# A hybrid decoder layer on one core: one group's block sums formed in device memory

## The chip, the cores and the metric

One core of a Trainium2 chip runs the whole layer as one program. The metric is the device time of one execution in microseconds. TensorE (PE) does the matrix products, VectorE (DVE) and ScalarE (ACT) the elementwise work, GpSimd (POOL) a few tiny operations and the accumulating transfers, SyncE (SP) issues plain transfers. The 16 DMA engines are shared by all queues. A transfer issued from POOL can add to its destination (`accum_op=ALU.add`); here these are called accumulates.

## The reference, cut to what matters

A decoder layer on 256 tokens of width 1024, all in fp32: a projection, block-sparse attention beside retention, an output projection, cross attention into 256 memory rows, and a gated FFN of inner width 2816, each with norms:

```python
h = rms_norm(x, g_pre_ffn[l])
gu = h @ w_gate_up[l]
f = (jax.nn.silu(gu[..., :D_FF]) * gu[..., D_FF:]) @ w_down[l]
x = x + rms_norm(f, g_post_ffn[l])
```

The change concerns the product with `w_gate_up`.

## The kernel before, in words

All weights lie in one array `weights` of blocks of 128 x 1024 fp32 (512 KB). Each block is used as two parts, high and low: ACT writes the high part (a copy to the rounded format, line 195), DVE the rest (line 196, a subtraction); this is a *split*, made by `split_weight`. PE then makes three products for each pair of operands (high x high, high x low, low x high). The blocks have numbers q in the order in which they are split (the table `SPLIT` sets it for the FFN); PE uses them in the order of `USE`. Split blocks lie in a ring of nine buffers, `hl`.

A block comes to its split in one of two ways. A *plain* one (kind `"w"`) is loaded by SP into a ring of six buffers, `raw`; `load_weight` issues the load for a later block when a split has freed a buffer. The others are *home* blocks, which stay in one of three tiles, `kT`, `qv` and `ret`, in SBUF.

Home blocks exist because of the *seven-product groups* 1 to 4. Each group covers 512 columns of the gate and of the up half for both tiles of 128 tokens. In place of eight products of quarter size, seven are made, from sums and differences of the quarters. With the quarters 11, 12, 21, 22, the weight operands are: product 1: 11; 2: 21; 3: 22; 5: 11+12; 7: 22+12 (with the signs taken in by the token operands); 6: 11+12+22; 4: 11+12+22+21. Each operand has two blocks (parts). Products of a group have the PE line 1167, with the accumulators x, y and z.

In a group the homes are loaded with three quarters and then changed in place: after its split a home block gets another quarter added, either by DVE (line 202, where the other quarter lies in a home) or by an accumulate that POOL issues (line 204). `load_home` (line 145) makes the first loads; group 1's are issued by SP, those of the later groups by POOL once the group before has read the home for the last time.

Side work (norms, softmax, the kernel's tails of a product) is written as generators that `run_side` resumes at numbered steps of PE's program; `late` starts some at a fixed step, and `WAIT` holds the delays in steps. A split is put off by a step in which side work was resumed, unless it is due. So a new generator can also move splits. All engines run their own instructions in order, and SP and POOL stop at a transfer that has to wait.

Of the kernel before, what the change touches and what calls it, by code (L numbers as in the profile page):

```python
# [7 lines left out]
F32 = mybir.dt.float32  # L8
F32R = mybir.dt.float32r
BF16 = mybir.dt.bfloat16  # L10
AF = mybir.ActivationFunctionType
ALU = mybir.AluOpType
AX = mybir.AxisListType

P = 128
D = 1024
# [6 lines left out]
FFN_Q = 64  # L23
HOMES = {1: ('kT', 'qv', 'ret', '21'), 2: ('qv', 'kT', 'ret', '21'), 3: ('qv', 'kT', 'ret', '21'), 4: ('qv', 'kT', 'ret', '12')}
SEVEN = tuple(HOMES)
# [2 lines left out]
USE = 'r20 r21 d0 d1 1:1 d2 1:2 1:5 1:6 1:3 d3 1:7 d20 1:4 2:1 d21 2:2 d4 2:5 2:6 2:3 2:7 d5 2:4 3:1 3:2 d6 d7 d9 d8 3:5 3:6 3:3 3:7 d10 3:4 d11 d12 d13 4:1 d14 4:2 4:5 4:6 4:3 4:7 d15 4:4'.split()  # L28
SPLIT = 'r20 r21 d0 1:1 d1 1:2 d2 1:5 1:3 1:6 d3 1:7 1:4 d20 2:1 2:2 d21 d4 2:5 2:3 2:6 2:4 2:7 d5 3:2 3:1 d6 d9 d7 d8 3:5 3:3 3:6 3:4 3:7 d10 d12 d11 d13 d14 4:1 4:5 4:2 4:6 4:3 d15 4:7 4:4'.split()
DOWN_END = (16, 17, 18, 19)  # L30
FIRST_OUT = (0, 512, 768, 1024)
ROW_TILES = tuple(int(what[1:]) for what in USE if what[0] == "r")
ROWS_AT = FFN_Q + 8
SEVEN_AT = ROWS_AT + 2 * len(ROW_TILES)
DOWN_AT = SEVEN_AT + 8 * len(SEVEN)

WAIT = {
    "cpb0": 2, "cpb1": 1, "cpv0": 7, "cpv1": 1, "cu0": 3, "cu1": 4, "ex_c0": 2, "ex_c1": 1, "ex_m00": 0,
    "ex_m10": 0, "ex_m11": 4, "f0_0": 8, "f0_1": 7, "g_add": 0, "g_silu": 5, "gate0": 3, "gate1": 6,
    "gp1": 5, "gp2": 0, "k_add": 0, "k_hl": 3, "lag": 2, "ret": 12, "low": 6, "mq": 0, "mrow": 3, "ms": 21, "mst": 5,  # L40
# [14 lines left out]
def tile_hybrid_layer(  # L55
# [14 lines left out]
    nc = tc.nc  # L70
# [3 lines left out]
    hlp = ctx.enter_context(tc.tile_pool(name="hlp", bufs=RING))  # L74
    rawp = ctx.enter_context(tc.tile_pool(name="rawp", bufs=RAW))
    stp = ctx.enter_context(tc.tile_pool(name="stp", bufs=1))
    t2k = ctx.enter_context(tc.tile_pool(name="t2k", bufs=7))
    p4 = ctx.enter_context(tc.tile_pool(name="p4", bufs=2))
    pt4 = ctx.enter_context(tc.tile_pool(name="pt4", bufs=3))
# [42 lines left out]
    emitted = set()  # L122

    def need(*keys):

        missing = [k for k in keys if k not in emitted]
        assert not missing, missing
# [7 lines left out]
    raws, hls = {}, {}  # L135

    items = [("w", q) for q in range(FFN_Q)]
    queue = []
    sums = {}

    def load_home(engine, g, home, part, w):

# [4 lines left out]
    def load_weight():  # L147

        if not queue:
            return  # L150
        q = queue.pop(0)
        kind, w = items[q][:2]
        if kind == "w":
            raws[q] = rawp.tile([P, D], F32, tag="raw", name=f"raw{q}")
            nc.sync.dma_start(raws[q], weights[w])
        else:
            for key in firsts[q]:
                if key[:2] not in follows:
                    load_home(nc.sync, *key)
            load_weight()  # L160

    homes = {}
    ringed = []
    split_at = {}
    ret_kept = [1000, 1000]
    beside = {}
    firsts, follows, released = {}, {}, {}

    def free_home(q, i):

        if len(ringed) < RING or last_use[ringed[-RING]] + WAIT["lag"] <= i:
            return "hl"
        if q >= FFN_Q and ("oT", 7, 1) in emitted:
            for tag in ("qv", "kT", "ret") if q < FFN_Q + 8 else ("ret",) if not ret_kept[0] - WAIT["ret"] < q <= ret_kept[1] else ():
                if tag not in homes or last_use[homes[tag]] + WAIT["lag"] <= i:
                    return tag
        return None

    def split_weight(q, parts=1, home="hl"):
        kind = items[q][0]  # L180
        if kind == "w":
            raw = raws.pop(q)
        else:
            g, tag, part = items[q][2:5]
            raw = sums[(g, tag)][:, part, :]
        if home == "hl":
            ringed.append(q)
            h = hlp.tile([P, 2, D], F32R, tag="hl", name=f"hl{q}")
        else:
            homes[home] = q  # L190
            h = actp.tile([P, 2, D], F32R, tag=home, name=f"hl{q}")
        w = D // parts
        for i in range(parts):
            n = slice(i * w, (i + 1) * w)
            nc.scalar.activation(h[:, 0, n], raw[:, n], AF.Copy)  # L195
            nc.vector.tensor_tensor(out=h[:, 1, n], in0=raw[:, n], in1=h[:, 0, n].bitcast(F32), op=ALU.subtract)  # L196
        hls[q] = h
        split_at[q] = step_no[0]
        if kind != "w":
            plus, more = items[q][5:7]  # L200
            if plus is not None:
                nc.vector.tensor_tensor(out=raw, in0=raw, in1=sums[(g, plus)][:, part, :], op=ALU.add)  # L202
            if more is not None:
                nc.gpsimd.dma_start(raw, weights[more], accum_op=ALU.add)
            for key in released.get(q, ()):
                load_home(nc.gpsimd if HOME_LOADS == "late-pool" else nc.sync, *key)
        if kind == "w":
            load_weight()
# [456 lines left out]
    parts = {}  # L665
# [154 lines left out]
    both = [(0, 1)]  # L820
# [45 lines left out]
    def seven_items(g, w0):  # L866

        b = {"11": w0, "12": w0 + 2, "21": w0 + 4, "22": w0 + 6}
        one, two, three = HOMES[g][:3]
        held = HOMES[g][3] if three else None  # L870
        here = g in ON_CHIP
        plus = {1: three if held == "12" else None, 5: two if here else None, 6: three if held == "21" else None,
                3: three if held == "12" else None}
        more = {1: "12", 5: "22", 6: "21", 3: "12"}
        chain = {m: (kind, w, home, plus.get(m), None if plus.get(m) else more.get(m))
                 for m, kind, w, home in ((1, "first", "11", one), (3, "first", "22", two), (5, "sum", None, one),
                                          (6, "sum", None, one), (7, "sum", None, two), (4, "sum", None, one))}
        if held == "21":
            chain[2] = ("first", "21", three, None, None)
        if held == "12":  # L880
            for part in range(2):
                beside[(g, one, part)] = (three, b["12"] + part)
        made = {(2, part): ("w", b["21"] + part) for part in range(2)}
        for m, (kind, source, home, plus, more) in chain.items():
            for part in range(2):
                made[(m, part)] = (kind, b[source] + part if source else None, g, home, part, plus,
                                   None if more is None else b[more] + part, m)
        return made
# [6 lines left out]
    place = {}  # L895
    made = {g: seven_items(g, SEVEN_AT + 8 * n) for n, g in enumerate(SEVEN)}
    for what in SPLIT + [f"d{k}" for k in DOWN_END]:
        if what[0] == "r":
            w = ROWS_AT + 2 * ROW_TILES.index(int(what[1:]))
# [5 lines left out]
    for what in USE:  # L905
# [4 lines left out]
        elif what[0] == "d":  # L910
            k = int(what[1:])
# [8 lines left out]
    for half in range(2):  # L920
        for q, k in blocks:
            steps.append(("down", q, 1, k // 4, k % 4, (half,)))
    NQ = len(items)
    kept = [q for q, item in enumerate(items) if item[0] != "w" and "ret" in (item[3], item[5])]
    if kept:
        ret_kept[:] = kept[0], kept[-1]

    loads, last_read = {}, {}
    for q, item in enumerate(items):
        if item[0] == "w":  # L930
            continue
        kind, w, g, home, part, plus = item[:6]
# [41 lines left out]
    qv = actp.tile([P, 2048], F32, tag="qv", name="qv")  # L974
# [72 lines left out]
    raw = raws.pop(0)  # L1047
# [12 lines left out]
    split_weight(1, 2)  # L1060
    x_split(2, 3)
    opening = {4: lambda: x_split(4, 5), 7: lambda: x_split(6, 7)}
    late = {WAIT["xd"]: x_load, WAIT["xs"]: x_stats, WAIT["ms"]: mem_stats}
    pending_split = list(range(2, NQ))

    accs, downs = {}, {}
    for i, s in enumerate(steps):
# [14 lines left out]
        if i == starts["ffn"]:  # L1082
            f = stp.tile([P, 2, 2, 4, 256], F32R, tag="stB", name="fT")
            T["fT"] = f
        if s[0] == "first":

            _, q, c = s
            need(("xT", q, 0))
            h = hls[q][:, :, c * 512:(c + 1) * 512]
# [211 lines left out]
```

## Time and profile before

| | |
|---|---|
| median of 3 timed runs | 400.16 us (399.66 to 400.49) |
| profiled execution | 398.5 us, of which the span is 396.7 us |
| PE busy | 389.1 us of the span |
| DVE busy | 320.5 us |
| ACT busy | 257.6 us |
| TensorE clock granted | 0.999 |
| SP queue (q1) | 62.97 MB, 45.1% of the DMA engines' span |
| POOL queue (q0) | 16.78 MB, 17.1% |

Stages, by the profile: input projection with attention and retention to about 111 us, keys and queries of the cross attention to 156 us, its values and output to about 215 us, FFN from there. A row of instructions has the line, engine, operation, output and inputs by the program's names, the form, the count, and the busy time or start; a share of DMA is the mean over the 16 engines.

### The profile page before, as it was taken

How to read it: one execution, taken by the hardware profiler on the slowest of the kernel's cores; microseconds unless marked ns; L12 is line 12 of the kernel's file. 1: busy time of each engine (PE TensorE's matmuls, PEld its weight loads, DVE VectorE, ACT ScalarE, POOL GpSimd, SP SyncE). 2: the span in 40 equal slices, each digit the busy share in tenths (PEclk: the TensorE clock that was granted, in tenths of full speed). 3: DMA queues.
4: the chain of work that ended last, by engine and by line, in shares of the span. 5: the costliest groups of instructions: out<-in, count | busy, mean ns of one | idle time of the engine just before them, and what ended most of it. 6: DMA issues, size and time to landing. Idle time of an engine off the chain costs nothing.

```text
span 396.7 us, 5465 instructions
## 1 busy us (share of the span) xinstructions
PE 389.1 (98%) x1969; PEld 323.8 (82%) x1969; DVE 320.5 (81%) x447; ACT 257.6 (65%) x431; POOL 33.4 (8%) x53
## 2 busy tenths in 40 slices
PE   8999999999999999999999999999999999999993
PEld 5888777888889888888988888888888888888882
DVE  4875976686869977677576699998999799999964
ACT  5786973964757865494547765757758685647641
POOL 0010010200011000000001001022113103101000
PEclk9999999999999999999999999999999999999999
DMA  8998746367546676607271459968949878935202
GB/s 280 415 401 274 253 159 212 106 207 275 168 152 240 184 218 204 213 6 240 74 265 55 159 191 359 299 104 315 241 120 274 245 241 178 366 146 121 40 0 106
DMA packets 23067, 80.36 MB, mean 203 GB/s; under 512 B 2560, under 2 KB 3072, under 8 KB 23040
## 3 DMA queue, kind: packets, MB, share of 16 engines
q1 hardware_dynamic: 18288, 62.97, 45.1%
q0 software_dynamic: 4608, 16.78, 17.1%
q8 instruction: 15, 0.25, 0.2%
q10 hardware_dynamic: 144, 0.26, 0.2%
q14 instruction: 12, 0.10, 0.1%
HBM read 78.95 MB, written 1.05 MB: 202 GB/s over the span
## 4 chain that ended last, share of the span: by engine, by line
PE 91%; DVE 3%; issue 2%; ACT 1%; DMA 1%; POOL 1%; DVEq 0%; POOLq 0%; ACTq 0%
PE x L1167 11%; PE acc L1107 11%; PE acc L1109 11%; PE acc L1108 11%; PE acc L1131 9%; PE y L1167 5%; PE acc L1134 5%; PE down L1152 5%; PE down L1154 5%; PE down L1153 5%; PE acc L1095 3%; PE z L1167 3%; DVE hl L196 1%; DMA raw<-in_weights_dram 1%; PE c_f L658 1%
## 5 line engine op out<-in xcount | busy, mean ns | idle before, releaser
L196 DVE TENSOR_TENSOR hl<-raw,hl 128x1024 fp32r<-128x1024 f32 (+1 forms) x102 | 119.3, 1189 | 16.9 <-ACT hl L195 16.8
L195 ACT ACTIVATE hl<-raw 128x1024 fp32r<-128x1024 f32 (+1 forms) x102 | 102.6, 1031 | 1.1 <-DMA raw<-in_weights_dram 1.0
L195 ACT ACTIVATE hl<-sum_qv 128x1024 fp32r<-128x1024 f32 x28 | 29.1, 1056 | 16.6 <-DVE sum_qv L202 12.1
L196 DVE TENSOR_TENSOR hl<-sum_qv,hl 128x1024 fp32r<-128x1024 f32 x28 | 34.0, 1220 | 1.4 <-ACT hl L195 1.3
L1107 PE MATMUL acc<-hl,xT 128*128 128x512 f32 x80 | 32.9, 411 | 0.0
L1109 PE MATMUL acc<-hl,xT 128*128 128x512 f32 x80 | 31.3, 392 | 0.0
L1152 PE MATMUL down<-hl,fT 128*128 128x512 f32 x80 | 31.3, 392 | 0.0
L1108 PE MATMUL acc<-hl,xT 128*128 128x512 f32 x80 | 31.2, 390 | 0.0
L1154 PE MATMUL down<-hl,fT 128*128 128x512 f32 x80 | 31.2, 390 | 0.0
L1153 PE MATMUL down<-hl,fT 128*128 128x512 f32 x80 | 31.2, 389 | 0.0
L196 DVE TENSOR_TENSOR hl<-sum_kT,hl 128x1024 fp32r<-128x1024 f32 x20 | 24.1, 1220 | 0.7 <-ACT hl L195 0.7
L1167 PE MATMUL x<-hl,x2T 128*128 128x512 f32 x96 | 23.2, 393 | 0.0
L1167 PE MATMUL x<-hl,comb 128*128 128x512 f32 x96 | 23.1, 390 | 0.0
L1167 PE MATMUL y<-hl,comb 128*128 128x512 f32 x96 | 23.1, 389 | 0.0
L1167 PEld LDWEIGHTS x<-hl,comb 128*128 128x128 f32 x96 | 17.9, 188 | 3.9 <-DVE hl L196 0.2
L1167 PEld LDWEIGHTS y<-hl,comb 128*128 128x128 f32 x96 | 18.0, 188 | 3.7
L195 ACT ACTIVATE hl<-sum_kT 128x1024 fp32r<-128x1024 f32 x20 | 20.5, 1051 | 0.5 <-DMA sum_kT<-in_weights_dram 0.5
L1167 PEld LDWEIGHTS x<-hl,x2T 128*128 128x128 f32 x96 | 17.7, 188 | 3.7 <-DVE s L685 0.2
L1154 PEld LDWEIGHTS down<-hl,fT 128*128 128x128 f32 x80 | 15.0, 188 | 3.3 <-DVE fT L661 0.2
L1109 PEld LDWEIGHTS acc<-hl,xT 128*128 128x128 f32 x80 | 15.0, 188 | 3.3
L1107 PEld LDWEIGHTS acc<-hl,xT 128*128 128x128 f32 x80 | 15.1, 189 | 3.1 <-issue 0.3
L1152 PEld LDWEIGHTS down<-hl,fT 128*128 128x128 f32 x80 | 15.0, 188 | 3.0
(258 smaller groups left out, 856.8 us busy)
## 6 DMA issues: line engine op xcount, KB each, us to landing
raw<-in_weights_dram SPq DMA_DIRECT2D x98, 512.0 KB, 4.9
sum_qv<-in_weights_dram POOLq DMA_DIRECT2D x14, 512.0 KB, 5.8
sum_kT<-in_weights_dram POOLq DMA_DIRECT2D x12, 512.0 KB, 6.8
sum_ret<-in_weights_dram POOLq DMA_DIRECT2D x6, 512.0 KB, 4.2
gpost<-in_gpost_dram SPq DMA_DIRECT2D x3, 512.0 KB, 4.9
x_sb<-in_x_dram SPq DMA_DIRECT2D x2, 512.0 KB, 8.2
memn<-in_mem_dram SPq DMA_DIRECT2D x2, 512.0 KB, 7.5
mr<-in_memT_dram SPq DMA_DIRECT2D x2, 512.0 KB, 7.4
```

The lines of the kernel that those rows point to most:

```text
L195: nc.scalar.activation(h[:, 0, n], raw[:, n], AF.Copy)
L196: nc.vector.tensor_tensor(out=h[:, 1, n], in0=raw[:, n], in1=h[:, 0, n].bitcast(F32), op=ALU.subtract)
L1095: nc.tensor.matmul(accs[(c, t)], T["xT"][:, hx, q, tok(t)], h[:, hw, :], start=begin, stop=False)
L1107: nc.tensor.matmul(acc, xh, h[:, 0, kk, :], start=(first and kk == 0), stop=False)
L1108: nc.tensor.matmul(acc, xh, h[:, 1, kk, :], start=False, stop=False)
L1109: nc.tensor.matmul(acc, xl, h[:, 0, kk, :], start=False, stop=(last and kk == 1))
L1131: nc.tensor.matmul(acc, hls[q][:, 0, k * P:(k + 1) * P], T[f"{st}_k"][:, k, :], start=begin, stop=end, skip_group_check=True)
L1134: nc.tensor.matmul(acc[:, 0:256], hls[q][:, 1, k * P:(k + 1) * P], T[st][:, 0, k, :], start=begin, stop=end, skip_group_check=True)
L1152: nc.tensor.matmul(acc, fh, wh, start=first, stop=False, skip_group_check=True)
L1153: nc.tensor.matmul(acc, fh, wl, start=False, stop=False, skip_group_check=True)
L1154: nc.tensor.matmul(acc, fl, wh, start=False, stop=last, skip_group_check=True)
L1167: nc.tensor.matmul(acc, a, h[:, w, kk, :], start=begin and kk == 0 and n == 0, stop=end and n == 2, skip_group_check=True)
```

## The change

Group 1 has no home blocks any more: all of its operands are plain blocks. Its sums are made ahead in device memory, in four scratch tensors of two blocks each. The new generator `make_sums` starts at step 70 (some 118 us in). For each sum it issues a copy of a quarter, or of an earlier sum, from device memory to device memory on SP, and later an accumulate of another quarter into the copy on POOL. The order is `PRE_ORDER`: copies for 5 and 7, accumulates for 5 and 7, copy of 5 to 6, accumulate of 22 into 6, copy of 6 to 4, accumulate of 21 into 4; two parts each, so eight copies and eight accumulates. A copy is followed by a delay of two steps, an accumulate by one of three. The blocks are then loaded through `raw` like weights (14 loads).

```diff
-FIRST_OUT = (0, 512, 768, 1024)
+PRE = (1,)
+PRE_ON = "sp"
+PRE_ORDER = "c5 c7 a5 a7 c6 a6 c4 a4".split()
+FIRST_OUT = (0, 256, 512, 640, 768, 1024)
...
 WAIT = {
+    "pre": 70, "pc": 2, "pa": 3,
...
+    dramp = ctx.enter_context(tc.tile_pool(name="dramp", bufs=1, space=bass.MemoryType.DRAM))
...
+    def make_sums():
+        for g in PRE:
+            at = SEVEN_AT + 8 * SEVEN.index(g)
+            w0 = {"11": at, "12": at + 2, "21": at + 4, "22": at + 6}
+            for what in PRE_ORDER:
+                m = int(what[1])
+                source, plus = {5: ("11", "12"), 7: ("22", "12"), 6: (5, "22"), 4: (6, "21")}[m]
+                for part in range(2):
+                    key = (g, m, part)
+                    if what[0] == "c":
+                        if part == 0:
+                            both = dramp.tile([P, 2, D], F32, tag=f"sum{g}{m}", name=f"sum{g}{m}")
+                        made_sums[key] = both[:, part, :]
+                        engine = nc.sync if PRE_ON == "sp" else nc.gpsimd
+                        engine.dma_start(made_sums[key], block((g, source, part) if isinstance(source, int) else w0[source] + part))
+                    else:
+                        nc.gpsimd.dma_start(made_sums[key], weights[w0[plus] + part], accum_op=ALU.add)
+                        emitted.add(("sum",) + key)
+                    yield WAIT["pc"] if what[0] == "c" else WAIT["pa"]
...
         if kind == "w":
+            if not isinstance(w, int):
+                need(("sum",) + w)
             raws[q] = rawp.tile([P, D], F32, tag="raw", name=f"raw{q}")
-            nc.sync.dma_start(raws[q], weights[w])
+            nc.sync.dma_start(raws[q], block(w))
...
     def seven_items(g, w0):
         b = {"11": w0, "12": w0 + 2, "21": w0 + 4, "22": w0 + 6}
+        if g in PRE:
+            plain = {1: "11", 2: "21", 3: "22"}
+            return {(m, part): ("w", b[plain[m]] + part if m in plain else (g, m, part)) for m in range(1, 8) for part in range(2)}
...
-    late = {WAIT["xd"]: x_load, WAIT["xs"]: x_stats, WAIT["ms"]: mem_stats}
+    late = {WAIT["pre"]: make_sums, WAIT["xd"]: x_load, WAIT["xs"]: x_stats, WAIT["ms"]: mem_stats}
```

`block(w)` gives `weights[w]` for a number and the scratch tensor for a key. `FIRST_OUT` cuts the output of the first token tile into pieces of columns. The rule by which a split may use a free home as a tenth buffer is also written for each home apart; the places in which it is used stay the same (three blocks of the first FFN products).

The order of PE's instructions does not change at all. Three places on the queues and on DVE do. SP, in the stage of the cross attention's queries and values, from before:

```order
L155 DMA raw_1532<-in_weights_dram 128x1024
L155 DMA raw_1555<-in_weights_dram 128x1024
L155 DMA raw_1586<-in_weights_dram 128x1024
L155 DMA raw_1609<-in_weights_dram 128x1024
L155 DMA raw_1640<-in_weights_dram 128x1024
```

and now (`sum_1262` holds operand 5, `sum_1579` operand 6, `sum_1714` operand 4):

```order
L188 DMA raw_1544<-in_weights_dram 128x1024
L188 DMA raw_1567<-in_weights_dram 128x1024
L166 DMA sum_1579<-sum_1262 128x1024
L188 DMA raw_1600<-in_weights_dram 128x1024
L166 DMA sum_1579<-sum_1262 128x1024
L188 DMA raw_1624<-in_weights_dram 128x1024
L188 DMA raw_1656<-in_weights_dram 128x1024
L188 DMA raw_1683<-in_weights_dram 128x1024
L188 DMA raw_1695<-in_weights_dram 128x1024
L188 DMA raw_1706<-in_weights_dram 128x1024
L166 DMA sum_1714<-sum_1579 128x1024 x2
L188 DMA raw_1824<-in_weights_dram 128x1024
```

Two copies for operand 6 (each waits for an accumulate into `sum_1262`) and two for operand 4 (each waits for one into `sum_1579`) now stand ahead of raw loads that only waited for a buffer. The load of before at the place of `raw_1600` was issued at 149.86 us, that at the place of `raw_1824` at 163.88 us.

POOL, from the first norm of the mixer to the cross attention's second norm, now (`sum_1323` holds operand 7):

```order
L258 TENSOR_TENSOR r_x_1279<-v_x_1277,mhalf 128x1
L168 DMA sum_1262<-in_weights_dram 128x1024 x2
L168 DMA sum_1323<-in_weights_dram 128x1024 x2
L168 DMA sum_1579<-in_weights_dram 128x1024 x2
L168 DMA sum_1714<-in_weights_dram 128x1024 x2
L258 TENSOR_TENSOR r_p_cross_2091<-v_p_cross_2089,mhalf 128x1
```

Before, `r_p_cross` followed `r_x` directly; now eight accumulates, which wait for SP's copies, stand between.

DVE in group 1, from the splits of operand 5 to those of operand 6, before:

```order
L196 TENSOR_TENSOR hl_2546<-sum_kT_2236,hl_2546 128x1024
L202 TENSOR_TENSOR sum_kT_2236<-sum_kT_2236,sum_qv_2317 128x1024
L196 TENSOR_TENSOR hl_2556<-sum_kT_2236,hl_2556 128x1024
L202 TENSOR_TENSOR sum_kT_2236<-sum_kT_2236,sum_qv_2317 128x1024
L196 TENSOR_TENSOR hl_2567<-sum_qv_2317,hl_2567 128x1024
L535 TENSOR_TENSOR f_2577<-sg_2429,f_2577 128x256
L614 TENSOR_TENSOR sg_2483<-sg_2483 128x256
L196 TENSOR_TENSOR hl_2589<-sum_qv_2317,hl_2589 128x1024
L196 TENSOR_TENSOR hl_2599<-sum_kT_2236,hl_2599 128x1024
L202 TENSOR_TENSOR sum_kT_2236<-sum_kT_2236,sum_ret_2282 128x1024
L196 TENSOR_TENSOR hl_2610<-sum_kT_2236,hl_2610 128x1024
L202 TENSOR_TENSOR sum_kT_2236<-sum_kT_2236,sum_ret_2282 128x1024
```

and now:

```order
L236 TENSOR_TENSOR hl_2565<-raw_2430,hl_2565 128x1024
L236 TENSOR_TENSOR hl_2576<-raw_2461,hl_2576 128x1024
L236 TENSOR_TENSOR hl_2588<-raw_2486,hl_2588 128x1024
L575 TENSOR_TENSOR f_2599<-sg_2444,f_2599 128x256
L654 TENSOR_TENSOR sg_2500<-sg_2500 128x256
L236 TENSOR_TENSOR hl_2611<-raw_2526,hl_2611 128x1024
L236 TENSOR_TENSOR hl_2622<-raw_2546,hl_2622 128x1024
L236 TENSOR_TENSOR hl_2634<-raw_2568,hl_2634 128x1024
```

The four additions of line 202 are gone from between the splits; the splits themselves stand in the same order and read raw buffers.

More of the change, by code (lines that the diff above doesn't have):

```diff
@@ L30 @@
 DOWN_END = (16, 17, 18, 19)
-FIRST_OUT = (0, 512, 768, 1024)
+BY_DMA = ()
+PRE = (1,)
+PRE_ON = "sp"
+PRE_ORDER = "c5 c7 a5 a7 c6 a6 c4 a4".split()
+FIRST_OUT = (0, 256, 512, 640, 768, 1024)
 ROW_TILES = tuple(int(what[1:]) for what in USE if what[0] == "r")
@@ L139, in tile_hybrid_layer, with block @@
     sums = {}
+    made_sums = {}
+    def block(w):
+        return weights[w] if isinstance(w, int) else made_sums[w]
+    def make_sums():
[17 more added lines that the diff above has]
+                    yield WAIT["pc"] if what[0] == "c" else WAIT["pa"]
     def load_home(engine, g, home, part, w):
@@ L162, in tile_hybrid_layer @@
     homes = {}
+    by_dma = set()
     ringed = []
     split_at = {}
-    ret_kept = [1000, 1000]
+    kept = {}
     beside = {}
@@ L173, in free_home @@
         if q >= FFN_Q and ("oT", 7, 1) in emitted:
-            for tag in ("qv", "kT", "ret") if q < FFN_Q + 8 else ("ret",) if not ret_kept[0] - WAIT["ret"] < q <= ret_kept[1] else ():
+            for tag in ("qv", "kT", "ret"):
+                if tag in kept and kept[tag][0] - WAIT["ret"] < q <= kept[tag][1]:
+                    continue
                 if tag not in homes or last_use[homes[tag]] + WAIT["lag"] <= i:
@@ L192, in split_weight @@
         w = D // parts
-        for i in range(parts):
+        if q in by_dma:
+            nc.scalar.activation(h[:, 1, :], raw, AF.Copy, scale=-1.0)
+            nc.scalar.activation(h[:, 0, :], raw, AF.Copy)
+            nc.gpsimd.dma_start(h[:, 1, :], block(items[q][1]), accum_op=ALU.add)
+        for i in range(parts) if q not in by_dma else ():
             n = slice(i * w, (i + 1) * w)
@@ L922, in tile_hybrid_layer @@
             steps.append(("down", q, 1, k // 4, k % 4, (half,)))
+    by_dma = {place[f"d{k}"] for k in BY_DMA}
     NQ = len(items)
-    kept = [q for q, item in enumerate(items) if item[0] != "w" and "ret" in (item[3], item[5])]
-    if kept:
-        ret_kept[:] = kept[0], kept[-1]
+    for tag in ("kT", "qv", "ret"):
+        used = [q for q, item in enumerate(items) if item[0] != "w" and tag in (item[3], item[5])]
+        if used:
+            kept[tag] = used[0], used[-1]
     loads, last_read = {}, {}
```

## The prediction

> **What bounds the kernel now.** I read the page's busy times first, then the idle time before TensorE's instructions, then the table of stages, then the chain of waits at its end.
>
> ```profile
> span 396.7 us, 5465 instructions
> ...
> PE 389.1 (98%) x1969; PEld 323.8 (82%) x1969; DVE 320.5 (81%) x447; ACT 257.6 (65%) x431; POOL 33.4 (8%) x53
> ```
>
> TensorE (PE) is busy for 98% of the span. Asked for what its matmuls waited for between 30 and 380 us, the trace gives one row:
>
> ```profile
> PE c_R_mem L247 <- POOL r_mem L218: 0.2, 1, 0.2
> ```
>
> So 0.2 us in 350. No change that only frees another engine can shorten that stretch by more, in this execution. The stages (columns: window, its length, busy us of PE, weight loads, DVE, ACT and POOL, TensorE clock, DMA share, GB/s):
>
> ```profile
> 10.00:30.00 20.00, 20.00 (x92) 16.55 (x91) 16.51 (x38) 16.07 (x24) 1.08 (x2) 1.00 1.02 405
> 126.00:163.00 37.00, 37.00 (x211) 32.39 (x210) 31.33 (x56) 24.57 (x48) 0.00 (x0) 1.00 0.62 189
> 163.00:181.00 18.00, 18.00 (x107) 15.96 (x106) 12.43 (x19) 11.19 (x24) 0.00 (x0) 1.00 0.34 122
> 181.00:200.00 19.00, 19.00 (x111) 16.72 (x111) 12.11 (x16) 11.01 (x16) 0.00 (x0) 1.00 0.42 134
> 240.00:280.00 40.00, 40.00 (x196) 33.71 (x196) 38.37 (x49) 26.17 (x37) 7.96 (x12) 1.00 0.85 267
> 280.00:320.00 40.00, 40.00 (x183) 32.89 (x182) 37.17 (x38) 27.70 (x33) 7.54 (x11) 1.00 0.83 217
> 320.00:360.00 40.00, 40.00 (x182) 32.99 (x181) 39.22 (x38) 24.93 (x30) 5.00 (x8) 1.00 0.66 212
> ```
>
> Two things stand here. PE is full in every stage, also where the DMA engines are full (10 to 30 us, 1.02, clock 1.00), so DMA traffic as such does not slow it. And in the FFN, from 240 us, VectorE (DVE) is nearly full too (38.37, 37.17, 39.22 of 40). How close the two come shows where PE first reads product 7 of groups 2, 3 and 4, whose blocks DVE has just split (pairs of DVE and PE rows):
>
> ```profile
> 302.06 2.47 DVE L196 TENSOR_TENSOR hl<-sum_kT,hl 128x1024 fp32r<-128x1024 f32 x2
> 303.18 2.96 PE L1167 MATMUL x<-hl,comb 128*128 128x512 f32 x12
> 335.56 2.48 DVE L196 TENSOR_TENSOR hl<-sum_kT,hl 128x1024 fp32r<-128x1024 f32 x2
> 336.86 1.75 PE L1167 MATMUL x<-hl,comb 128*128 128x512 f32 x7
> 369.09 2.35 DVE L196 TENSOR_TENSOR hl<-sum_kT,hl 128x1024 fp32r<-128x1024 f32 x2
> 370.51 1.75 PE L1167 MATMUL x<-hl,comb 128*128 128x512 f32 x7
> ```
>
> The first of each pair of splits ends at about 303.3, 336.8 and 370.3; PE starts at 303.18, 336.86 and 370.51. DVE is just in time. What that cost can be read in the chain of waits:
>
> ```profile
> 300.62 2.72 PE y L1167 x12
> 303.34 2.80 PE x L1167 x12
> ...
> 384.34 0.24 PE down L1154
> ...
> 392.38 0.75 DVE x_sb L782
> ```
>
> Twelve matmuls take 2.72 us, and 2.80 where DVE was just late: 0.08 us lost. After PE's last products the chain is the final norm and the output, about 4 us that the sums do not touch.
>
> The profiled execution took 398.5 us, 1.8 us around its span; the median of the timed runs is 400.16, 1.66 us above it. I make the sum against 398.5 and add it to 400.16.
>
> **The change, step by step.** *Sums removed from VectorE.* Group 1's four additions go:
>
> ```profile
> L202 DVE TENSOR_TENSOR sum_kT<-sum_kT,sum_qv 128x1024 f32<-128x1024 f32 x2 | 2.5, 1226 | 0.1
> L202 DVE TENSOR_TENSOR sum_kT<-sum_kT,sum_ret 128x1024 f32<-128x1024 f32 x2 | 2.5, 1225 | 0.1
> ```
>
> 4 x 1.226 = 4.9 us of DVE, between 257 and 268 us. PE does not wait there, so on the path this is worth nothing but slack: DVE comes to 302 us up to 4.9 us earlier, and the 0.08 us there goes. At 336 and 370 us the PE rows show nothing to win. The splits themselves stay (14 in number, from raw tiles instead of sums).
>
> *Sixteen transfers added early.* Eight copies on SP and eight accumulates on POOL, each 512 KB. At the 405 GB/s of the 10 to 30 us row a plain transfer takes 512 KB / 405 = 1.29 us of all DMA engines; a copy from device memory to device memory is not in this trace: between 1.29 and twice that, 2.6. For accumulates (here into SBUF) the page of line L204, and for the engines' share the window 290 to 303 us:
>
> ```profile
> DMA to landing us min/median/max: 5.3/6.6/9.7
> ...
> q0 software_dynamic: 390, 1.46, 57.6%
> ```
>
> 57.6% of 13 us for 1.46 MB (2.8 transfers of 512 KB) is 2.7 us each. I take 1.29 and 2.7, the nearest rows: 8 x 1.29 + 8 x 2.7 = 32 us; at the upper ends (2.6, and 5.3 if the destination in device memory doubles it) 63 us. Free DMA time between 126 and 200 us is 0.38 x 37 + 0.66 x 18 + 0.58 x 19 = 37 us. So at my price the engines are nearly full there, at the upper one the work runs on past 230 us; PE needs the first sum at 264 us. What hides it is the lead of the raw loads:
>
> ```profile
> raw<-in_weights_dram SPq DMA_DIRECT2D x25, 512.0 KB, 4.1
> ...
> raw<-in_weights_dram SPq DMA_DIRECT2D x5, 512.0 KB, 14.6
> ```
>
> The first row is 105 to 180 us, the second 235 to 247 us, where the engines are full: loads landed after 14.6 us there, and PE did not wait. If all raw loads of 126 to 200 us took 14.6 instead of 4.1, each would come 10.5 us later. Cost taken: 0; if that lead were gone, up to those 10.5 us.
>
> *The new waits.* SP is in order, so raw loads queue behind a copy that waits. The copy for product 6 waits for the accumulate for 5, the one for 4 for the accumulate for 6; on POOL the accumulates wait for the copies. The rows of before at these places:
>
> ```profile
> 125.25 0.66 POOL L218 TENSOR_TENSOR r_x<-v_x,mhalf 128x1 f32<-128x1 f32 x1 [4.64 <-DVE v_x L214]
> 147.06 0.33 SPq L155 DMA_DIRECT2D raw<-in_weights_dram  x1
> 163.88 0.33 SPq L155 DMA_DIRECT2D raw<-in_weights_dram  x1
> 189.41 1.05 ACT L195 ACTIVATE hl<-raw 128x1024 fp32r<-128x1024 f32 x1
> 201.14 0.39 PE L1107 MATMUL acc<-hl,oT 128*128 128x512 f32 x1
> 205.74 0.55 POOL L218 TENSOR_TENSOR r_p_cross<-v_p_cross,mhalf 128x1 f32<-128x1 f32 x1 [79.83 <-DVE v_p_cross L216]
> ```
>
> POOL is free for the first accumulate at 125.9, its copy, issued at about 120, has landed by 130 even at 9.7 us. The accumulate lands by 139.7; SP reaches the copy for 6 after the raw load of 147.06: no wait. That copy's second part goes out at about 150, has landed by 154 to 160, its accumulate by 161 (6.6) to 169 (9.7). SP reaches the copy for 4 just before the load of 163.88: no wait at the median, 5.4 us at the maximum. The load behind it is split at 189.41 (the ACT row) and first read by PE at 201.14: nothing comes of 5.4 us. On POOL, r_p_cross of 205.74 stands behind the last accumulates, which can be issued once the copies for 4 have landed, by 179: 26 us to spare. Cost 0; from below 0, since nothing here starts sooner for it; from above the rival of the slow links.
>
> The Trainium skill, "DMA: Bandwidth & Descriptors", section on the anatomy of one DMA, warns that a transfer's completion can be surprisingly long delayed, above all when it writes to device memory; all sixteen new transfers do. The only such writes in this trace say otherwise (rows next), but they are small and at an idle time, so the rule keeps a chance as the rival of the slow links.
>
> ```profile
> out_dram<-x_sb SPq DMA_DIRECT2D x3, 256.0 KB, 2.0
> ```
>
> *Group 1's loads.* Fourteen raw loads take the place of six loads and four accumulates: 14 x 1.29 = 18.1 us of DMA against 6 x 1.29 + 4 x 2.7 = 18.5, no difference. SP issues eight more, 8 x 0.33 us on a queue that mostly waits. Group 2's first loads move from POOL to SP and earlier, since the homes are free; nothing there is late. One split around 178 to 184 us moves three steps (4 us) later, PE reads it at 198 or after: 0. The first token tile's output goes out in five pieces instead of three; SP issues from 387.7, has until 393.1, and a piece costs it at most 0.46 us: 0, bounds minus and plus 0.1.
>
> **Sum:** minus 0.08 us: 398.4 on the profiled execution, 400.1 on the median; with the slack that DVE gains I write 400.0, no change. Bounds: minus 0.3 (0.08 and the 0.2 us of waits), and plus 1.4, one block of 1.36 us late once where the early transfers crowd the engines.
>
> **Rivals.** *Faster.* The timed runs' 1.66 us above the profiled one could be PE waiting for DVE at the three meeting points, where any lateness of DVE is PE's at once. Then 4.9 us of DVE slack frees the first point wholly, and the others as far as the lead lasts. If two of three go, 1.1 us: 399.0; if all, 398.5. For it: those pairs of rows. Against it: PE shows 0.2 us of waits in all, and the 1.66 may as well lie around the span.
>
> *Slower: the links are slow.* If an accumulate takes long and the six that SP depends on follow each other from 130 us, SP stands until 130 + 6d. The load behind must go out by 201.14 - (4.1 + 1.05 + 1.22) = 194.8, so it decides from d = 10.8 us, just over the 9.7 of the slowest here. At 12 us SP is free at 202: 7.2 us, 407.4.
>
> *Slower: group 1's blocks come late.* They now pass the ring of six raw buffers, so a load goes out six splits ahead. PE needs one every 2.72 / 2 = 1.36 us. Lead at product 5:
>
> ```profile
> 254.22 1.22 DVE L196 TENSOR_TENSOR hl<-sum_kT,hl 128x1024 fp32r<-128x1024 f32 x1
> 264.28 2.72 PE y L1167 x12
> ```
>
> 264.28 - 255.44 = 8.8 us. With loads landing after 14.6 us a block comes every 14.6 / 6 = 2.43 us, and (2.43 - 1.36) x 14 - 8.8 = 6.2 us: 406.4. It decides from 1.36 + 8.8 / 14 = 1.99 us a block, a latency of 11.9. Against it: those 14.6 us stood behind six home loads in a row (6 x 1.29 = 7.7 us), which are gone there.
>
> **How the numbers follow.** About 0.2% (0.8 us) is what a measurement of this kernel tells from no change. No change 0.57, its own range 399.4 to 401.0; faster 0.28, from 398.5 to 399.4; slow links 0.06; late blocks 0.09. The range 398.6 to 401.4 (400.0 plus the 1.4) leaves out the two slower rivals and the last of the faster one, 0.17.
>
> **What would show it.** In the profile after: L202 rows with four additions fewer; PE still 389 us and without waits from 30 to 380; at product 7 of group 2 more than 1 us between DVE's split and PE's read. DMA share from 126 to 200 us near 0.9. The prediction is wrong if SP waits for an accumulate beyond 185 us, if ACT waits for raw tiles in group 1 and PE after it, or if the time falls although PE's row stays full.

## The result, and the profile after

The changed kernel takes 401.69 us (median of 8 runs, 401.22 to 402.07); the kernel before, beside it, 399.62 us (8 runs, 398.93 to 400.96). The ratio is 1.0053, with a 95% interval of 1.0040 to 1.0066: half a per cent slower, clear of the noise, where no change was forecast, and just outside the range. The profiled execution has a span of 399.8 us, 3.1 us more than that of before. The medians differ by less, 2.07 us, since the profiled execution of before (398.5 us) was faster than any of its eight runs here.

The page after, first lines and busy times:

```profile
span 399.8 us, 5499 instructions
...
PE 390.7 (98%) x1969; PEld 324.3 (81%) x1969; DVE 315.7 (79%) x443; ACT 257.2 (64%) x431; POOL 33.1 (8%) x51
```

DVE lost 4.8 us of work (4 instructions), as the change intends. What PE's matmuls waited for between 30 and 380 us:

```profile
PE x L1212 <- DVE hl L236: 2.1, 3, 1.0
PE c_R_mem L287 <- POOL r_mem L258: 0.2, 1, 0.2
```

The second row was there before. The first is new: three waits, 2.1 us, for a split by DVE. PE's weight loads, which come first, wait longer for the same three:

```profile
PEld x L1212 <- DVE hl L236: 3.3, 3, 1.4
```

(Lines up to the group code are 40 higher than in before, later ones 45: L236 was L196, L1212 was L1167.) The stages place it:

```profile
126.00:163.00 37.00, 37.00 (x211) 32.40 (x211) 31.18 (x56) 24.89 (x48) 5.16 (x7) 1.00 1.02 322
163.00:181.00 18.00, 18.00 (x108) 15.95 (x106) 11.78 (x18) 10.03 (x23) 1.62 (x2) 1.00 0.96 244
181.00:200.00 19.00, 19.00 (x113) 16.75 (x112) 12.69 (x16) 11.84 (x17) 0.00 (x0) 1.00 0.62 187
240.00:280.00 40.00, 40.00 (x197) 33.72 (x196) 34.17 (x46) 25.69 (x36) 1.77 (x2) 1.00 0.80 282
280.00:320.00 40.00, 37.94 (x171) 30.41 (x170) 34.20 (x34) 24.83 (x31) 6.80 (x11) 1.00 0.83 234
```

From 126 to 181 us, where the sums are formed, the DMA engines are as good as full (1.02, 0.96), and PE loses nothing there or in the row behind. It loses 2.06 us between 280 and 320, in group 2, whose splits, sums and products the change does not touch. PE's rows there:

```profile
297.92 0.39 PE L1212 MATMUL x<-hl,comb 128*128 128x512 f32 x1
299.27 1.65 PE L1212 MATMUL x<-hl,comb 128*128 128x512 f32 x6 [0.96 <-DVE hl L236]
301.67 1.42 PE L1212 MATMUL x<-hl,comb 128*128 128x512 f32 x5 [0.74 <-DVE hl L236]
...
306.42 2.79 PE L1212 MATMUL x<-hl,comb 128*128 128x512 f32 x11 [0.36 <-DVE hl L236]
```

The first two waits are at the two parts of product 6, the third at product 7, whose accumulates into `sum_kT` POOL issued at 296.9 us instead of 293.6. The chain of waits goes back from there (start, length, what):

```profile
278.25 0.85 POOL sum_qv L244
279.11 12.50 DMA sum_qv<-in_weights_dram
...
291.63 1.07 ACT hl L235
...
293.99 1.22 DVE sum_qv L242
295.21 1.15 DVE hl L236
...
296.91 0.84 POOL sum_kT L244
...
297.78 7.23 DMA sum_kT<-in_weights_dram
```

An accumulate into `sum_qv` (11+12 for product 5 of group 2) takes 12.50 us to land. ACT cannot split the block before that; DVE, which splits it next and then adds for product 6, stands still. ACT's rows of that product's two parts, before and then after:

```profile
284.98 1.06 ACT L195 ACTIVATE hl<-sum_qv 128x1024 fp32r<-128x1024 f32 x1 [0.51 <-DMA sum_qv<-in_weights_dram]
...
288.55 1.06 ACT L195 ACTIVATE hl<-sum_qv 128x1024 fp32r<-128x1024 f32 x1 [0.44 <-DMA sum_qv<-in_weights_dram]
```

```profile
287.92 1.06 ACT L235 ACTIVATE hl<-sum_qv 128x1024 fp32r<-128x1024 f32 x1 [3.27 <-DMA sum_qv<-in_weights_dram]
...
291.63 1.06 ACT L235 ACTIVATE hl<-sum_qv 128x1024 fp32r<-128x1024 f32 x1 [1.68 <-DMA sum_qv<-in_weights_dram]
```

Both are some 3 us later, though POOL issued the pair of accumulates no later: at 278.23, and before at 278.55 and 279.88. From here ACT's rows stay late by the same 3.1 us, and PE's after its three waits; it is the size by which the span grew. What else was on the DMA engines? The SP queue from 264 us, before (all of its rows to 292 us) and after:

```profile
268.92 16.75 SPq L155 DMA_DIRECT2D raw<-in_weights_dram  x4
```

```profile
264.18 0.33 SPq L188 DMA_DIRECT2D raw<-in_weights_dram  x1
264.56 0.91 SPq L176 DMA_DIRECT2D sum_qv<-in_weights_dram  x2
265.57 1.45 SPq L176 DMA_DIRECT2D sum_ret<-in_weights_dram  x2
267.12 3.28 SPq L188 DMA_DIRECT2D raw<-in_weights_dram  x2
270.45 0.90 SPq L176 DMA_DIRECT2D sum_kT<-in_weights_dram  x2
271.45 13.93 SPq L188 DMA_DIRECT2D raw<-in_weights_dram  x6
```

Thirteen of these fifteen loads (6.8 MB) are issued ahead of the accumulates, within 14 us. Before it was eight (4.2 MB): two of the four raw loads, and group 2's six first loads, which were on POOL's queue from 267 to 276 us. The five additional ones are blocks of the down projection (94, 99, 100, 111 and 116, by the order in which the ring serves them): before, the first three were issued by 240 us, and 111 and 116 at 246 and 254. Blocks 117 and 118 are issued here in both kernels, and 119 behind the accumulates in both (283.91 us now). Now group 1's fourteen plain blocks pass through the ring of six raw buffers, so the down blocks get a buffer only when group 1's last splits free one, from 264.18 on, one behind the other. Beside the three places named under "The change", then, the order on the queues changes in a fourth: group 2's first loads are on SP now, not on POOL, and these down blocks stand among and behind them. What the queues moved between 264 and 279 us (packets, MB, share of the engines), before and after:

```profile
q0 software_dynamic: 1053, 3.85, 82.8%
q1 hardware_dynamic: 146, 0.53, 9.1%
```

```profile
q1 hardware_dynamic: 1484, 5.41, 95.5%
```

Before, 4.38 MB: about as much as had been issued. After, 5.41 of 6.8 MB: at least 1.4 MB still stood ahead when the accumulates came. Count and median time to landing of the accumulates and of the raw loads issued between 278 and 292 us, before and after:

```profile
sum_qv<-in_weights_dram POOLq DMA_DIRECT2D x2, 512.0 KB, 7.5
raw<-in_weights_dram SPq DMA_DIRECT2D x2, 512.0 KB, 5.7
```

```profile
sum_qv<-in_weights_dram POOLq DMA_DIRECT2D x2, 512.0 KB, 11.1
raw<-in_weights_dram SPq DMA_DIRECT2D x2, 512.0 KB, 8.7
```

My theory, called T1 in what follows, is *crowding*: the loads that the change delays lie just ahead of group 2's first accumulates on the shared DMA engines. The rivals are that forming the sums is what costs (in the early stage, or by what it leaves behind), and that the new output pieces cost at the end.

### The profile page after: what moved, and what is told of

It is laid out like the page before. It is cut to its first block, busy times and chain, and to the rows that moved or that the text cites. A ratio compares the mean times of both kernels' runs of the same rounds, so it can differ in the third digit from the quotient of the medians.

```text
span 399.8 us, 5499 instructions
## 1 busy us (share of the span) xinstructions
PE 390.7 (98%) x1969; PEld 324.3 (81%) x1969; DVE 315.7 (79%) x443; ACT 257.2 (64%) x431; POOL 33.1 (8%) x51
## 4 chain that ended last, share of the span: by engine, by line
PE 82%; DMA 5%; DVE 5%; issue 3%; ACT 3%; POOL 1%; DVEq 0%; POOLq 0%; ACTq 0%
PE acc L1152 11%; PE acc L1154 11%; PE acc L1153 11%; PE acc L1176 9%; PE x L1212 8%; PE acc L1179 5%; PE down L1199 4%; PE down L1197 4%; PE down L1198 4%; PE y L1212 3%; DMA sum_qv<-in_weights_dram 3%; PE acc L1140 3%; DVE hl L236 3%; PE z L1212 2%; DMA sum_kT<-in_weights_dram 2%
## 5 line engine op out<-in xcount | busy, mean ns | idle before, releaser
L236 DVE TENSOR_TENSOR hl<-raw,hl 128x1024 fp32r<-128x1024 f32 (+1 forms) x116 | 136.0, 1194 | 23.1 <-ACT hl L235 22.9
L235 ACT ACTIVATE hl<-raw 128x1024 fp32r<-128x1024 f32 (+1 forms) x116 | 116.7, 1034 | 2.1 <-DMA raw<-in_weights_dram 2.0
L235 ACT ACTIVATE hl<-sum_qv 128x1024 fp32r<-128x1024 f32 x24 | 24.7, 1056 | 17.3 <-DVE sum_qv L242 12.1
L236 DVE TENSOR_TENSOR hl<-sum_qv,hl 128x1024 fp32r<-128x1024 f32 x24 | 29.1, 1221 | 4.4 <-ACT hl L235 4.3
L1212 PE MATMUL x<-hl,comb 128*128 128x512 f32 x96 | 23.9, 393 | 2.1 <-DVE hl L236 2.1
L1212 PEld LDWEIGHTS x<-hl,comb 128*128 128x128 f32 x96 | 17.8, 188 | 6.9 <-DVE hl L236 3.3
L1212 PE MATMUL x<-hl,x2T 128*128 128x512 f32 x96 | 23.2, 393 | 0.0
L1212 PE MATMUL y<-hl,comb 128*128 128x512 f32 x96 | 23.1, 389 | 0.0
L1212 PEld LDWEIGHTS y<-hl,comb 128*128 128x128 f32 x96 | 18.0, 188 | 3.8
L1212 PEld LDWEIGHTS x<-hl,x2T 128*128 128x128 f32 x96 | 17.8, 188 | 3.7
L1199 PEld LDWEIGHTS down<-hl,fT 128*128 128x128 f32 x80 | 15.0, 188 | 3.3 <-DVE fT L701 0.2
L1152 PEld LDWEIGHTS acc<-hl,xT 128*128 128x128 f32 x80 | 15.1, 189 | 3.2 <-issue 0.3
L1154 PEld LDWEIGHTS acc<-hl,xT 128*128 128x128 f32 x80 | 15.0, 188 | 3.3
L1197 PEld LDWEIGHTS down<-hl,fT 128*128 128x128 f32 x80 | 15.0, 188 | 3.1
L1198 PEld LDWEIGHTS down<-hl,fT 128*128 128x128 f32 x80 | 15.0, 188 | 3.0
L1153 PEld LDWEIGHTS acc<-hl,xT 128*128 128x128 f32 x80 | 15.1, 189 | 2.6
```

Source lines behind the costliest of these rows:

```text
L1152: nc.tensor.matmul(acc, xh, h[:, 0, kk, :], start=(first and kk == 0), stop=False)
L1153: nc.tensor.matmul(acc, xh, h[:, 1, kk, :], start=False, stop=False)
L1154: nc.tensor.matmul(acc, xl, h[:, 0, kk, :], start=False, stop=(last and kk == 1))
L1197: nc.tensor.matmul(acc, fh, wh, start=first, stop=False, skip_group_check=True)
L1198: nc.tensor.matmul(acc, fh, wl, start=False, stop=False, skip_group_check=True)
L1199: nc.tensor.matmul(acc, fl, wh, start=False, stop=last, skip_group_check=True)
```

## The experiments

All ratios are to the kernel before, run beside it on the same chip.

**Forming alone.** The sums are formed, but group 1 still comes from homes.

```diff
-PRE = (1,)
+PRE = ()
+FORM = (1,)
...
-        for g in PRE:
+        for g in FORM:
```

> The changed kernel with group 1 taken back to home blocks and VectorE's sums; the eight copies and eight accumulates into device memory still run early, and nothing reads them. Theory of the crowded accumulate (group 2's first accumulates into sum_qv land late because plain loads of later blocks share the DMA engines with them at 278 to 291 us): the early transfers cost nothing, ratio to before 1.000 (0.998 to 1.002), no PE wait after 30 us. Rival, early crowding (the sixteen transfers between 120 and 186 us are what costs): ratio 1.005, with PE or ACT waiting before 200 us.

Measured: 401.61 us, ratio 1.0059 (1.0044 to 1.0074), against T1's expectation. The trace shows that this kernel is not the one I meant. A split that DVE makes at 203.01 us in before is missing there and comes at 225.09, where DVE makes two in a row instead of one, and TensorE's weight loads wait for it (DVE's rows of before and of this run, then the waits of its weight loads at 225 us and of its matmuls at 283 us):

```profile
203.01 1.22 DVE L196 TENSOR_TENSOR hl<-raw,hl 128x1024 fp32r<-128x1024 f32 x1 [0.26 <-ACT hl L195]
```

```profile
225.09 2.36 DVE L237 TENSOR_TENSOR hl<-raw,hl 128x1024 fp32r<-128x1024 f32 x2 [0.57 <-ACT hl L236]
```

```profile
PEld acc L1154 <- DVE hl L237: 0.6, 1, 0.6
...
PE x L1213 <- DVE s L726: 1.2, 1, 1.2
```

The changed rule for free homes, written for a group 1 without homes, keeps an ordinary split out of a home when group 1 still has them. So the run mixes two edits, and says nothing on forming. The larger wait, 1.2 us, comes at 283 us, behind a wait of ACT of 2.80 us for group 2's first *load* into `sum_qv` (2.23 us in before). How much of that follows from the late split was not taken apart. The clean form follows below.

**Loading alone.** The copies and accumulates are left out; quarter 12 is loaded in the place of each sum, so the four sums are not computed. Everything else is the changed kernel.

```diff
-                        made_sums[key] = both[:, part, :]
+                        made_sums[key] = weights[w0["12"] + part]
...
-                        engine.dma_start(made_sums[key], ...)
...
-                        nc.gpsimd.dma_start(made_sums[key], weights[w0[plus] + part], accum_op=ALU.add)
```

> The changed kernel without the sixteen transfers: group 1's four sum operands are loaded from the quarter 12 in the weights instead (the sums are left out, everything else is issued the same). Crowded accumulate: ratio 1.005 (1.003 to 1.007), PE waits about 2 us between 297 and 309 us, ACT waits some 5 us for sum_qv, as in the changed kernel. Early crowding, or loads from scratch memory being slower than from the weights: ratio 1.000.

Measured: 401.05 us, ratio 1.0048 (1.0033 to 1.0062). The loss is there without any of the sixteen transfers, by T1's figure for the time; PE waits 1.1 us for splits of group 2, half of what T1 expected.

**Down blocks held back.** The loads of five down blocks go out on POOL, behind group 2's first accumulates. Four of them (111, 116, 117, 118) lay ahead of the accumulates on SP; the fifth, 119, was issued behind them already.

```diff
+    HELD = (111, 116, 117, 118, 119)
...
+        (nc.gpsimd if q in HELD else nc.sync).dma_start(raws[q], block(w))
...
+            if q in HELD and 96 not in split_at:
+                held.append((q, w))
...
+            if q == 96:
+                for late_one in held:
+                    load_raw(*late_one)
```

> The changed kernel with five loads of down blocks (those split after 305 us) taken from SP and issued by POOL behind group 2's first accumulates, in the same queue. Crowded accumulate: the accumulates issued at 278 us land by about 285 and 288 instead of 288 and 291.6, PE's wait falls from 2.1 to under 0.5 us, ratio 1.000 (0.998 to 1.002). Rival, the home loads (group 2's six first loads, now on SP at 264 to 271 us, hold the queue, the down blocks do not matter): ratio stays at 1.004 to 1.006.

Measured: 398.74 us, ratio 0.9985 (0.9976 to 0.9994). The loss is gone. Landing in the same window, and ACT's two splits, now with no wait at all:

```profile
raw<-in_weights_dram POOLq DMA_DIRECT2D x5, 512.0 KB, 10.8
sum_qv<-in_weights_dram POOLq DMA_DIRECT2D x2, 512.0 KB, 6.7
```

```profile
284.93 1.05 ACT L245 ACTIVATE hl<-sum_qv 128x1024 fp32r<-128x1024 f32 x1
...
288.57 1.06 ACT L245 ACTIVATE hl<-sum_qv 128x1024 fp32r<-128x1024 f32 x1
```

It is now the raw loads that take 10.8 us, and nobody waits for them: they stand behind the accumulates, and are split from 303 us on.

**Group 2's first loads ahead.** They go out on SP at step 146 (241 to 245 us) instead of 264 to 271 us.

```diff
+    def homes_ahead():
+        for q, item in enumerate(items):
+            if item[0] == "first" and item[2] == 2:
+                for key in firsts[q]:
+                    load_home(nc.sync, *key)
+        yield 0
...
-    late = {WAIT["pre"]: make_sums, ...}
+    late = {146: homes_ahead, WAIT["pre"]: make_sums, ...}
```

> The changed kernel with group 2's six first loads issued by SP 20 us earlier (about 243 us), where the homes are free already. Crowded accumulate: the queue of loads at 264 to 290 us is 6 x 1.27 = 7.6 us shorter, the down blocks land before about 283 us, the accumulates land about 3 us earlier, ratio 0.998 to 1.002. Rival, the home loads: the same, 1.000. Rival, the down blocks alone, whose issue times do not change: the accumulates are as late as in the changed kernel, ratio 1.004 to 1.006.

Measured: 398.97 us, ratio 0.9995 (0.9982 to 1.0007). With the queue emptier by six transfers the down blocks issued from 271 us on land in 3.9 to 4.5 us each, the last at about 281 us; the accumulates take 8.8 us, and PE waits 0.4 us. So either part of the crowd can be moved away; only with both in the place are the accumulates late enough to cost time.

**The crowd alone, in the kernel before.** Six idle copies of 512 KB on SP's queue, issued from 278.16 to 281.46 us.

```diff
+        if q == 99:
+            for n in range(6):
+                if n % 2 == 0:
+                    idle = dramp.tile([P, 2, D], F32, tag=f"idle{n}", name=f"idle{n}")
+                nc.sync.dma_start(idle[:, n % 2, :], weights[n])
```

> The kernel before, with nothing of the change, to which six copies of 512 KB from device memory into an unused tile there are added on SP's queue behind the load at split 99, so that they run about 277 to 283 us, when group 2's first accumulates into sum_qv run. T1 (crowding: the accumulates that product 5 of group 2 waits for share the DMA engines with plain transfers queued just ahead of them): ACT's wait for sum_qv grows by 2 to 4 us, PE then waits for hl at the sixth product of group 2, and the time goes to 401 to 403 us, ratio 1.004 to 1.009, without any of the change. Rival (the sums' own work, or the plain form of group 1, makes the change slow): the accumulates land as in before, ratio 0.999 to 1.002.

Measured: 404.42 us, ratio 1.0133 (1.0109 to 1.0157). The kernel before can be made slow in the same place without any of the change. ACT's wait for the accumulates and loads of `sum_qv` from 270 to 330 us, and the landing of the accumulates:

```profile
ACT hl L196 <- DMA sum_qv<-in_weights_dram: 11.1, 7, 4.0
```

```profile
sum_qv<-in_weights_dram POOLq DMA_DIRECT2D x2, 512.0 KB, 11.3
```

The size was missed: I expected at most 1.009. The copies' queue holds the engines until 296.75 us (the last one's landing), beyond the pair of accumulates; and DVE still makes the sums of group 1 here, so it may have less slack. The trace names two more parts (a row of before, then two of this run, then the stages behind them):

```profile
280.82 5.30 PEld L1167 LDWEIGHTS x<-hl,x2T 128*128 128x128 f32 x24 [0.16 <-DVE s L685]
```

```profile
283.26 5.78 PE L1173 MATMUL x<-hl,x2T 128*128 128x512 f32 x24 [1.03 <-DVE s L691]
302.79 4.25 PE L1173 MATMUL x<-hl,comb 128*128 128x512 f32 x11 [2.17 <-DVE hl L197]
```

```profile
302.00:304.00 2.00, 1.21 (x3) 1.02 (x4) 1.97 (x3) 0.00 (x0) 0.16 (x1) 0.64 0.92 166
304.00:306.00 2.00, 2.00 (x7) 1.48 (x6) 1.97 (x2) 1.92 (x3) 0.00 (x0) 0.50 1.10 205
```

The wait of 1.03 us comes ahead of product 5 of group 2, and its cause is older than the copies: ACT waits 3.60 us for group 2's first load into `sum_qv`, issued at 272.60 us and landed as the first copy was issued. The wait of 2.17 us is the one that T1 forecast, at product 6. Behind it the granted TensorE clock was 0.64 and then 0.50, and eleven matmuls took 4.25 us; in the changed kernel eleven took 2.79 at 306.42 us, at a clock of 1.00. So only a part of the 4.9 us is the accumulates' lateness itself.

**Forming alone, clean.** As the first run, with the rule for homes of before. PE then runs the instructions of before in the order of before, and so do ACT and DVE but for one split at about 180 us, which the new side work moves some steps later, as in the changed kernel.

```diff
-            for tag in ("qv", "kT", "ret"):
-                if tag in kept and kept[tag][0] - WAIT["ret"] < q <= kept[tag][1]:
-                    continue
+            for tag in ("qv", "kT", "ret") if q < FFN_Q + 8 else ("ret",) if not kept["ret"][0] - WAIT["ret"] < q <= kept["ret"][1] else ():
```

> The sums are formed early as in the changed kernel, but nobody reads them: group 1 still comes from homes, and the rule that gives homes to ordinary splits is that of before, so that PE, DVE and ACT have the same instructions in the same order as before (in the form-only run that rule was the new one, and with group 1 at home it kept ordinary splits at 200 to 225 us from a home, which moved one split late). T1: the late split was that run's loss of 2.3 us, and forming the sums is free: 399.0 to 399.8 us, ratio 0.999 to 1.002. Rival (the forming transfers themselves cost time): 401 us or more, ratio 1.004 to 1.007, with a PE wait at 118 to 240 us that before has not.

Measured: 399.82 us, ratio 1.0006 (0.9994 to 1.0019). Forming costs nothing that can be measured (the interval allows 0.8 us at most), with the engines as full as in the changed kernel:

```profile
126.00:163.00 37.00, 37.00 (x210) 32.31 (x209) 30.87 (x56) 24.27 (x48) 5.06 (x6) 1.00 1.03 320
163.00:181.00 18.00, 18.00 (x108) 15.95 (x107) 11.31 (x19) 10.52 (x24) 1.61 (x2) 1.00 0.94 236
```

**Both cures.** Down blocks held and first loads ahead.

> The changed kernel with both cures: the five loads of down blocks wait on POOL's queue behind group 2's first accumulates, and group 2's six first loads go out at step 146. T1: each cure alone already took the wait away (ratios 0.9985 and 0.9995), so both give 398.3 to 399.0 us, ratio 0.997 to 0.9995. Rival (the gains add, since each took a different part): 398.0 us or less, ratio 0.997 or less.

Measured: 399.01 us, ratio 0.9988 (0.9976 to 1.0000). They do not add, as T1 said: the accumulates land in 6.4 us, and PE has no wait left in that place.

**The output pieces of before.** `FIRST_OUT = (0, 512, 768, 1024)` in the changed kernel.

> The changed kernel with the three output pieces of before instead of five. T1 and the prediction: the pieces change nothing, so the time is that of the changed kernel: 401.0 to 402.0 us, ratio 1.004 to 1.0066. Rival (two more transfers delay the end): 0.5 us or more less than the changed kernel, ratio 1.003 or less. Rival in the other sense (the finer pieces help the end): ratio above 1.007.

Measured: 401.47 us, ratio 1.0053 (1.0037 to 1.0069), the ratio of the changed kernel to the digit. The pieces show no effect.

**Two blocks held.** Only blocks 117 and 118 (`HELD = (117, 118)`).

> The changed kernel with only two of the five held loads (blocks 117 and 118, d9 and d7, which the changed kernel issues at 274.1 and 276.6 us) put on POOL's queue behind group 2's first accumulates; d5 and d6 (271.5 and 273.0 us) stay where they are. If what slows the accumulates is the transfers queued just ahead of them (T1), most of the loss goes with these two: 398.9 to 400.3 us, ratio 0.999 to 1.002, ACT's wait for sum_qv 1 to 3 us in 270 to 330. Rival (it needs the whole burst moved, because the queue as a whole is what is late): 400.7 us or more, ratio 1.003 or more.

Measured: 399.23 us, ratio 0.9984 (0.9972 to 0.9996). It gave the whole gain in time, a little more than T1's range of ratios (0.999 to 1.002), though not in landing: the accumulates still take 9.1 us, and ACT waits 4.3 us in all, where T1 expected 1 to 3. Here DVE's lead was nearly enough: PE waited 0.4 us.

**Two blocks held, in the kernel before.** The same edit, with nothing of the change.

> The kernel before, with nothing of the change, but with its loads of blocks 117 and 118 (issued on SP at 268.9 and 276.7 us) on POOL's queue behind group 2's first accumulates. It tells whose the gain of the held run (ratio 0.9985 to before) is. If it is that of the changed kernel's early sums, once the crowd is gone, this run shows nothing: ratio 0.9995 to 1.0005. If it is the crowd's alone, which before has in part (ACT waits 4.3 us for sum_qv there), this run is as fast: ratio 0.998 to 0.9993, 398.7 to 399.2 us beside a before of 399.5.

Measured: 398.52 us, ratio 0.9967 (0.9953 to 0.9981), better than either expectation, and the fastest of all. Its seven runs lie between 398.40 and 398.86, where the kernel before, beside it, ran from 398.46 to 400.83 (median 399.67). ACT makes its two splits at 284.52 and 288.17 us without a wait; the waits of 0.51 and 0.44 us in the profile of before are gone. So a gain as large as that of the held kernels is to be had without the early sums. Where it lies is not shown: the two profiled executions have spans of 396.9 us and, before, 396.7, so the 1.15 us between the medians belong to executions of before that no trace holds. Put side by side, the median landing of the two accumulates (in one profiled execution each) and the ratio:

| kernel | accumulates land in | ratio |
|---|---|---|
| before, two blocks held | 6.2 us | 0.9967 |
| before, sums formed (the clean form) | 6.3 us | 1.0006 |
| changed, both cures | 6.4 us | 0.9988 |
| changed, five blocks held | 6.7 us | 0.9985 |
| before | 7.5 us | 1 |
| before, sums formed, one split late (the first form) | 7.6 us | 1.0059 |
| changed, first loads ahead | 8.8 us | 0.9995 |
| changed, two blocks held | 9.1 us | 0.9984 |
| loading alone | 10.1 us | 1.0048 |
| changed, old output pieces | 11.0 us | 1.0053 |
| changed | 11.1 us | 1.0053 |
| before, with idle copies | 11.3 us | 1.0133 |

Between 9.1 and 10.1 us lies the point from which a changed kernel loses. Below it the order of the rows is not the order of the times: the clean forming run has the accumulates as early as any and gains nothing on before, and the first one loses elsewhere. The cured forms of the changed kernel stay at 0.9984 to 0.9988, the held kernel before is at 0.9967; on the same chip the two with two blocks held took 399.23 and 398.52 us. What these 0.7 us are stays open: the intervals overlap, and the early sums alone showed no cost.

## Why the prediction was wrong, point by point

- *Where it failed.* The step "Group 1's loads" of the prediction put the moved loads at nothing because it compared amounts: 18.1 us of DMA against 18.5, "no difference". The amounts were right (from 240 to 280 us the engines' share was 0.80, before 0.85), the time was not. It said of group 2's first loads that "nothing there is late", and asked only whether they would be in time. They were; what they and the down blocks among and behind them delayed was the accumulates of group 2, which landed after 11.1 us instead of 7.5 and cost PE 2.1 us by the waits of its matmuls, 3.3 us by those of its weight loads. The prediction followed the ring of raw buffers only for group 1's own blocks (its rival of the late blocks), not for the blocks that come through the same ring next. That rival did not happen: PE waits for no raw tile, and all the 2.1 us lie in group 2. None of the three signs of being wrong that the prediction named came, either: it failed where it had not looked.
- *No change, by slack.* "DVE comes to 302 us up to 4.9 us earlier" failed with it. DVE did have 4.8 us less to do, but stood still for the missing accumulates; it began product 6's parts of group 2 at 298.00 and 300.39 us, and product 7's at 305.14, not before 302.06.
- *The range's upper end,* 401.4, stood on one block late once (1.36 us). It had no term for a late accumulate; three waits came in a row behind one.
- *The sums' price* was right: the new transfers took (1.02 - 0.62) x 37 + (0.96 - 0.34) x 18 + (0.62 - 0.42) x 19 = 30 us of all DMA engines, forecast 32, and the mean share from 126 to 200 us was 0.90, as forecast. The clean run shows no cost in time.
- *The new waits* were there, and larger than I said, but without effect. SP's wait, by the trace, and what stood behind POOL's last accumulate:

```profile
SPq L166 <- DMA sum<-in_weights_dram: 7.5, 2, 4.3
```

```profile
205.94 0.56 POOL L258 TENSOR_TENSOR r_p_cross<-v_p_cross,mhalf 128x1 f32<-128x1 f32 x1 [28.39 <-DVE v_p_cross L256]
```

I had written no wait at the median and 5.4 us at the maximum; SP stood 7.5 us, in two waits for the copies for product 4. The copies for product 6 did not wait, as forecast. The 28 us of idle time on POOL ahead of `r_p_cross` are the cover that I named (26).
- *The rival of the slow links* needed accumulates of 10.8 us, one behind the other. They came close, and it did not decide:

```profile
DMA to landing us min/median/max: 6.3/9.6/10.7
```

  The Trainium skill, "DMA: Bandwidth & Descriptors", section on the anatomy of one DMA, warns of long completions of writes to device memory. The row bears it out in part: 9.6 us at the median, against 6.8 for the accumulates into SBUF in this trace, but on engines that were full.
- *The faster rival* was half right. It held that the timed runs of before lie above the profile because PE meets DVE at the edge. The run with two blocks held shows that such an excess exists (398.52 against 399.67 in the median) and can be had; but by moving two loads, not by taking sums off DVE. That it is had by landing the accumulates sooner is not shown: the clean forming run has them after 6.3 us and takes 399.82 us.
- *The tail:* 0, as forecast.

## What to carry to other kernels

When a change moves loads, follow the buffers' ring past the blocks in question: list what now gets its buffer late, when it is issued, and which transfer with a waiting reader is issued just behind it. Equal bytes are no argument; a burst ahead of a transfer on the path can cost time, here 2.07 us for five more loads of 512 KB in the 14 us ahead. A prefetch that nobody needs for 30 us is better issued behind the transfer that an engine waits for than ahead of it.

## What the runs showed of the hardware

Three kernels that differ only in plain transfers (before, before with two blocks held, before with idle copies) had the same two 512 KB accumulates land in 7.5, 6.2 and 11.3 us. And DMA engines that were full for 55 us (share 1.02 and 0.96, while most of the 8 copies and 8 accumulates inside device memory ran) took nothing from TensorE, at a granted clock of 1.00. In the run with idle copies a wait of 2.17 us on TensorE was followed by some 4 us at a granted clock of 0.64 and 0.50; behind the changed kernel's waits of at most 0.96 us the clock stayed at 1.00. In these runs the crowd cost time where a transfer with a waiting reader stood in it, and nowhere else that the traces show.
